# Weight sums of two Strassen projections: written to HBM ahead of time, or added in place in SBUF by accumulating transfers

## The chip, the cores and the metric

The kernel runs on one core of a Trainium2 chip. The metric is the device time of one execution in microseconds (us). The engines are named as in the profile: PE (TensorE, matmuls), DVE (VectorE), ACT (ScalarE), POOL (GpSimd) and SP (SyncE, which only issues transfers here). Each engine works through its own instructions in order and waits for others by semaphores. A transfer that POOL issues goes through the queue that the profile calls software_dynamic; one that SP issues goes through a hardware_dynamic queue.

## The reference, cut to what matters

The kernel computes one decoder block in float32, with 1024 tokens and a model width of 1024. Two mixers (an SSD branch and a gated linear attention branch, GLA) are each projected up, gated and added; the sum goes through w_o and is added to x. Then a cross attention begins with a projection through w_xq.

```python
y_ssd = ssd_mixer(z, xBC, dt_raw, ...)
y_gla = gla_mixer(q, k, v, r, a1, ...)
merged = sigmoid(g_ssd) * (y_ssd @ w_up_ssd) + sigmoid(g_gla) * (y_gla @ w_up_gla)
h = h + merged @ w_o
q = rmsnorm(h, norm_xattn) @ w_xq        # then scores against the memory, softmax, w_xo, the FFN
```

The change touches `merged @ w_o` and the product with `w_xq`, and what runs ahead of them.

## The kernel before

**Matmuls.** A float32 product is made from three matmuls of float32r parts: each operand is split into a high part (rounded by ACT) and a low part (DVE subtracts the high one), and hi x hi, hi x lo and lo x hi are added in PSUM. Arrays lie with the features on the 128 partitions and the tokens along the free side, in two token halves of 512.

**The order of the work.** A tile scheduler sets each engine's order from the program, by its own estimate of times and by priorities; code under `ahead()` is pulled forward, transfers wrapped in `pinned` keep the program's order. Stages here: the w_in projections beside the GLA chunks (`run(singles(...), (gla, ...))`, to about 803 us), dense(0) (y_ssd through w_up_ssd), dense(1) (y_gla through w_up_gla, to 986.8), the w_o product (`wo.steps()`), and the w_xq product (`xq.steps()`). `run` takes a step of each side generator per main step at a given rate.

**GLA.** There are 8 chunks. The last step of each, `norm`, transposes the chunk on PE (`bank<-ident,o`), copies it by ACT into `qk` and stores it by SP to HBM (`yg_d<-qk`). dense(0) first reads `hl<-ys_d` and its weights `raw<-in_w_up_ssd`, which ACT and DVE split into `wd`; the second `wd` buffer lies in memory that GLA's last `qk` held, so its split waits for that store. ACT also evaluates gates (`whi`, `wlo` loaded from `gs_d`).

**Wide.** The class `Wide` does a 1024 x 1024 x 1024 product by seven products of quarters (Strassen-Winograd). Each product is 48 matmuls of 128x512, in two halves of 24 that have an operand pair each (`ws`: a weight part and an activation part, both split into hi and lo). The left operand of B11, B21 and T4 is a quarter of W; those of T1, B22, T2 and T3 are sums of quarters, which the kernel has made ahead of time in HBM: `weight_sums` issues 12 transfers on POOL (copies first, then `accum_op=ALU.add` in halves of 512 KB), for w_o into `wos_d` during the GLA stage and for w_xq into `xqs_d` during dense(1). `Wide.load` then reads all seven left operands by SP as blocks of 1 MB (`wr`), three from W and four from the sums. `prep` forms the activation sums on DVE (`rq`) and splits both operands; `steps` runs three operand pairs ahead of PE; `evac` adds each product into `wk` on DVE, and for finished rows calls `post`: `post_wo` stores the row, scales it for w_xq (`put_xq`, ACT) and sums its square (`Stats.take`: ACT squares, POOL or DVE adds into `ssum`). `post_yg`, called for each of the 16 row blocks of dense(1), gates the row and adds the SSD part on POOL (`rq<-..,ga`), which yields w_o's activations.

Of the kernel before, what the change touches and what calls it, by code (L numbers as in the profile page):

```python
# [78 lines left out]
def block_kernel(ctx: ExitStack, tc: tile.TileContext, t: dict, out: bass.AP):  # L79
# [38 lines left out]
    wos_d = dram("wos_d", 2 * D, HALF)  # L118
    xqs_d = dram("xqs_d", 2 * D, HALF)
# [1101 lines left out]
    class Wide:  # L1221
# [4 lines left out]
        SEQ = ("B11", "T1", "B22", "T2", "B21", "T3", "T4")  # L1226
        LEFT = {"B11": (0, 0), "B21": (0, 1), "T1": 0, "B22": 3, "T2": 1, "T3": 2, "T4": (1, 1)}
# [5 lines left out]
        def __init__(s, W, sums_d, post, keys, side, base=None, scale=1.0, two=None):  # L1233
            s.W, s.sums_d, s.post, s.keys, s.side, s.base, s.scale = W, sums_d, post, keys, side, base, scale
            s.two = two or (lambda ap: DVE)
            s.q, s.raw, s.ops, s.keep, s.chain = {}, [], [], {}, None
# [18 lines left out]
        def home(s, i, j):  # L1255
            if (i, j) not in s.keep:
                k = s.keep[i, j] = slot(s.side[len(s.keep)], (P, 4, HALF), name="wk")
                if s.base is not None:
                    pinned(SP.dma_start(k, s.base[half(i), half(j)].rearrange("(u p) c -> p u c", p=P)))
            return s.keep[i, j]  # L1260

        def prep(s, n, pin=None):
            pin = pin or (lambda x: x)
            while len(s.ops) < min(n, 14):
                m, kp = divmod(len(s.ops), 2)
                s.load(m + 1)
                name, c = s.SEQ[m], slice(2 * kp, 2 * kp + 2)
                x = [slot("op", (P, 2, 2, HALF), F32R, name="ws") for _ in range(2)]
                with ahead():
                    if name in s.COMB:  # L1270
                        f, *q = s.COMB[name]
                        o, a, b = (s.quad(*ij)[:, c] for ij in q)
# [634 lines left out]
```

## Time and profile before

| What | us |
| --- | --- |
| Median of 3 runs | 1937.14 |
| Lowest and highest of them | 1934.5, 1938.31 |
| The profiled execution, its own time | 1939.03 |
| Its span in the trace | 1937.3 |
| PE busy in it | 1898.9 (98%) |
| DVE, ACT, POOL busy | 1359.5, 882.1, 533.6 |

All durations below are from that one profiled execution, whose own time is 1.9 us above the median of the runs. A row of a timeline gives when an operation started, how long it took, and in brackets how long its engine had stood before it and what ended that. Windows give the busy time of each engine in a stretch, the share of full speed that PE's clock was granted, and how busy the DMA engines were (1.0 is all 16; a row can come out a little above it).

### The profile page before, as it was taken

What the parts mean: (1) busy time and instruction counts of PE and PEld (TensorE: products, weight loads), DVE (VectorE), ACT (ScalarE), POOL (GpSimd) and SP (SyncE); (2) the same over time, 40 slices, a digit from 0 to 9 for tenths busy, and PEclk for the clock granted to TensorE, in tenths of its full rate; (3) what the DMA queues carried; (4) which work ended last, traced back from release to release, by engine and by line L of the source; (5) the groups of instructions that cost most, each with busy time, mean ns of one, the idle gap of its engine ahead of it and who ended that gap; (6) DMA issues with size and microseconds to landing.
All of it is one profiled execution on the core that took longest, in us unless ns stands there. A gap on an engine that the chain in (4) does not pass through costs nothing.

```text
span 1937.3 us, 26098 instructions
## 1 busy us (share of the span) xinstructions
PE 1898.9 (98%) x9680; PEld 1600.8 (83%) x9680; DVE 1359.5 (70%) x1935; ACT 882.1 (46%) x1521; POOL 533.6 (28%) x426
## 2 busy tenths in 40 slices
PE   7999999999999999899999999999999999999998
PEld 7998787888888888788888888888888888888888
DVE  7765879877776665552288685687878877866566
ACT  7534564555553444652236564553333333345243
POOL 0012324345443322001322100016544534330002
PEclk9999999999999999899999999999999999999999
DMA  9433383456653966984874420424675557397463
GB/s 343 145 94 102 126 303 117 146 164 183 185 163 121 271 193 182 338 288 161 227 202 159 170 85 12 156 94 130 181 194 147 147 166 182 101 298 264 159 222 121
DMA packets 242915, 341.04 MB, mean 176 GB/s; under 512 B 16458, under 2 KB 147764, under 8 KB 242788
## 3 DMA queue, kind: packets, MB, share of 16 engines
q1 hardware_dynamic: 225572, 293.23, 45.0%
q0 software_dynamic: 15488, 39.85, 9.8%
q10 hardware_dynamic: 1728, 6.29, 0.8%
q8 instruction: 76, 1.25, 0.3%
q14 instruction: 51, 0.42, 0.1%
HBM read 249.87 MB, written 129.30 MB: 196 GB/s over the span
## 4 chain that ended last, share of the span: by engine, by line
PE 85%; DVE 7%; DMA 3%; issue 2%; ACT 1%; POOL 1%; SPq 0%; POOLq 0%; DVEq 0%; ACTq 0%
PE acc L51 69%; PE bank L51 14%; DVE cv L73 2%; PE bank L55 2%; DVE wlo L73 2%; DVE o L73 1%; DVE hs L73 1%; DMA yg_d<-qk 1%; DMA hl<-ys_d 0%; DMA qk<-q_d 0%; DMA raw<-in_w_ffn_in_dram 0%; DMA down_d<-in_w_ffn_out_dram 0%; POOL ssum L73 0%; ACT cv L778 0%; DVE gy L73 0%
## 5 line engine op out<-in xcount | busy, mean ns | idle before, releaser
L73 DVE TENSOR_TENSOR wlo<-raw,whi 128x512 fp32r<-128x512 f32 x272 | 243.6, 903 | 97.3 <-ACT whi L233 97.3
L233 ACT ACTIVATE whi<-raw 128x512 fp32r<-128x512 f32 x272 | 169.7, 630 | 253.1 <-PE acc L51 208.8
L51 PE MATMUL acc<-hl,wd 128*128 128x512 f32 x1152 | 266.9, 393 | 6.5 <-ACT wd L233 6.5
L51 PEld LDWEIGHTS acc<-hl,wd 128*128 128x128 f32 x1152 | 217.7, 190 | 54.0 <-ACT wd L233 8.3
L73 DVE TENSOR_TENSOR o<-acc,o 128x512 f32<-128x512 f32 x244 | 166.9, 684 | 82.2 <-PE acc L51 80.5
L51 PE MATMUL acc<-fs 128*128 128x512 f32 (+1 forms) x792 | 155.7, 355 | 0.1
L51 PEld LDWEIGHTS acc<-fs 128*128 128x128 f32 x792 | 130.7, 189 | 20.8 <-issue 0.5
L73 DVE TENSOR_TENSOR fs<-fr,fs 128x1024 fp32r<-128x1024 f32 (+1 forms) x78 | 93.0, 1225 | 36.2 <-ACT fs L233 36.1
L233 ACT ACTIVATE fs<-fr 128x1024 fp32r<-128x1024 f32 (+1 forms) x78 | 74.1, 983 | 94.4 <-PE acc L51 29.2
L73 POOL TENSOR_TENSOR sa<-raw 128x512 f32<-128x512 f32 x42 | 68.3, 1625 | 149.2 <-DMA raw<-in_w_in_dram 80.3
L233 ACT ACTIVATE whi<-sa 128x512 fp32r<-128x512 f32 x96 | 59.7, 626 | 96.1 <-PE acc L51 90.5
L51 PE MATMUL acc<-ws 128*128 128x512 f32 x384 | 88.8, 390 | 0.0
L73 POOL TENSOR_TENSOR raw<-raw,sa 128x512 f32<-128x512 f32 x33 | 44.8, 1357 | 155.7 <-DVE wlo L73 155.7
L51 PEld LDWEIGHTS acc<-ws 128*128 128x128 f32 x384 | 71.9, 188 | 15.2 <-DVE ws L73 0.3
L73 DVE TENSOR_TENSOR wlo<-sa,whi 128x512 fp32r<-128x512 f32 x96 | 72.7, 757 | 8.4 <-ACT whi L233 7.5
L51 PE MATMUL acc<-T4h,whi 128*128 128x512 f32 x192 | 75.9, 395 | 2.6 <-DVE o L73 2.6
L51 PE MATMUL acc<-T3h,whi 128*128 128x512 f32 x192 | 75.7, 394 | 2.0 <-DVE o L73 2.0
L51 PE MATMUL acc<-B22h,wlo 128*128 128x512 f32 x192 | 75.8, 395 | 1.6 <-DVE wlo L73 1.6
L73 POOL TENSOR_TENSOR rstd<-rstd,mhalf 128x4 f32<-128x4 f32 (+1 forms) x7 | 8.7, 1250 | 247.8 <-DVE rstd L73 247.8
L51 PE MATMUL acc<-T1h,whi 128*128 128x512 f32 x192 | 76.3, 397 | 0.0
L51 PE MATMUL acc<-T2h,whi 128*128 128x512 f32 x192 | 75.8, 395 | 0.0
L51 PE MATMUL acc<-B22h,whi 128*128 128x512 f32 x192 | 75.7, 394 | 0.0
(420 smaller groups left out, 5039.2 us busy)
## 6 DMA issues: line engine op xcount, KB each, us to landing
raw<-in_w_in_dram SPq DMA_DIRECT2D x26, 1024.0 KB, 7.8
raw<-in_w_ffn_in_dram SPq DMA_DIRECT2D x22, 1024.0 KB, 6.7
act_d<-o SPq DMA_DIRECT2D x77, 256.0 KB, 3.3
fr<-act_d SPq DMA_DIRECT2D x35, 512.0 KB, 5.6
down_d<-in_w_ffn_out_dram POOLq DMA_DIRECT2D x18, 768.0 KB, 7.3
fr<-down_d SPq DMA_DIRECT2D x20, 512.0 KB, 4.1
ga<-h_d SPq DMA_DIRECT2D x32, 256.0 KB, 6.8
csb<-cs_d SPq DMA_DIRECT2D x15, 512.0 KB, 4.2
```

The costliest lines, as they stand in the source:

```text
L51: return s.e.matmul(o, x, y, **kw)
L55: return s.e.transpose(o, x, i)
L73: return f(*a, **kw)
L233: pin(ACT.activation(hi, src, AF.Copy))
```

## The change

The HBM buffers `wos_d` and `xqs_d` and the 24 transfers that filled them are gone from the GLA stage and from dense(1). Each `Wide` now loads five blocks by SP: B11's, B21's, T1's, T3's and T4's. Where a left operand is a sum, POOL adds another quarter of W onto a loaded block in SBUF by accumulating transfers, each in two halves of 512 KB (`plus`). T1's block A10 gets A11 at once. T2's sum is made in T1's buffer, each half after T1's split of that half has read it; B22's in the same buffer after T2's split; T3's block A00 gets A10 in a buffer of its own. The products run in a new order, B11, B21, T1, T2, B22, T3, T4; for w_o the two token halves change roles (`flip=1`); buffers have other homes. The 16 additions of `post_yg` move from POOL to DVE. The side generator of cross attention (`xq_side`) waits three steps instead of two.

```diff
-    wos_d = dram("wos_d", 2 * D, HALF)
-    xqs_d = dram("xqs_d", 2 * D, HALF)
...
-    def dense_sums(w, d):
-        return weight_sums([(t[w].rearrange("(j k p) c -> j p k c", j=2, p=P), d, 4, 0)])
-
     gla = gla_steps()
-    wsums = dense_sums("w_o", wos_d)
-    run(singles(gs[2:] + gg[:3], B, gg[3:]), (gla, 8 * 5 / 30), (wsums, 0.37), prio=PRIO)
+    run(singles(gs[2:] + gg[:3], B, gg[3:]), (gla, 8 * 5 / 30), prio=PRIO)
     drain(gla)
-    drain(wsums)
...
-        SEQ = ("B11", "T1", "B22", "T2", "B21", "T3", "T4")
-        LEFT = {"B11": (0, 0), "B21": (0, 1), "T1": 0, "B22": 3, "T2": 1, "T3": 2, "T4": (1, 1)}
+        SEQ = ("B11", "B21", "T1", "T2", "B22", "T3", "T4")
+        LEFT = {"B11": (0, 0), "B21": (0, 1), "T1": (1, 0), "T3": (0, 0), "T4": (1, 1)}
+        PLUS = {"T1": (1, 1), "T2": (0, 0), "B22": (0, 1), "T3": (1, 0)}
...
-        def load(s, n):
-            while len(s.raw) < min(n, 7):
-                src = s.LEFT[s.SEQ[len(s.raw)]]
-                if isinstance(src, tuple):
-                    i, j = src
-                    w = s.W[half(j), half(i)]
-                else:
-                    w = s.sums_d[half(src), :]
-                r = slot(s.keys[len(s.raw)], (P, 4, HALF), name="wr")
-                pinned(SP.dma_start(r, w.rearrange("(k p) c -> p k c", p=P)))
-                s.raw.append(r)
...
+        def block(s, i, j):
+            return s.W[half(j), half(i)].rearrange("(k p) c -> p k c", p=P)
+
+        def plus(s, name, k):
+            r = s.raw[name][:, k:k + 2]
+            pinned(POOL.dma_start(r, s.block(*s.PLUS[name])[:, k:k + 2], accum_op=ALU.add))
+
+        def load(s, *names):
+            for name in names:
+                if name in s.raw:
+                    continue
+                r = s.raw[name] = slot(s.keys.get(name, s.keys["*"]), (P, 4, HALF), name="wr")
+                pinned(SP.dma_start(r, s.block(*s.LEFT[name])))
+                if name in s.PLUS:
+                    for k in (0, 2):
+                        s.plus(name, k)
...
         def prep(s, n, pin=None):
...
                 m, kp = divmod(len(s.ops), 2)
-                s.load(m + 1)
                 name, c = s.SEQ[m], slice(2 * kp, 2 * kp + 2)
+                if name in s.LEFT:
+                    s.load(name)
...
+                if name in ("T1", "T2"):
+                    s.raw[s.SEQ[m + 1]] = s.raw[name]
+                    s.plus(s.SEQ[m + 1], 2 * kp)
                 s.ops.append(x)
...
-            first = name in ("B11", "T1", "B22")
+            first = name in ("B11", "T1", "T2")
...
                 for kp in range(2):
-                    s.load(m + 3)
+                    if 2 * m + kp in (0, 7):
+                        s.load("T4" if m else "T3")
                     s.prep(x + 3)
...
         gated(g, p)
-        q = wo.quad(o // 4, j)[:, o % 4]
-        add(POOL, q, g, y)
+        add(DVE, wo.rows(o, j), g, y)
...
-    wo = Wide(t["w_o"], wos_d, post_wo, ("aux",) * 7, ("m", "m", "m", "aux"), xT_d, 0.5)
+    wo = Wide(t["w_o"], post_wo, {"B21": "m", "*": "aux"}, {(0, 0): "m", (0, 1): "m", (1, 1): "m", (1, 0): "aux"}, xT_d, 0.5, flip=1)
...
-    wsums = dense_sums("w_xq", xqs_d)
-    run(dense(1, i_yg, post_yg, lambda o, j: (gate(gg_d, o, j), quad(ysg_d, o * P, 0, j))), (wide_side(wo, 8, 4, pinned), 1.0), (wsums, 0.8))
-    drain(wsums)
-    run(wo.steps(), (wide_side(xq, 7, 2), 1.0))
+    run(dense(1, i_yg, post_yg, lambda o, j: (gate(gg_d, o, j), quad(ysg_d, o * P, 0, j))),
+        (wide_side(wo, (("T1", 8), ("B11", 10), ("B21", 12)), (13, 14), pinned), 1.0))
+    run(wo.steps(), (wide_side(xq, (("T1", 6), ("B11", 7), ("B21", 8)), (11, 12)), 1.0))
```

The scheduler moves work at places far from the edit, too. On SP's queue at the end of GLA and the start of dense(0) these rows stand, first before, then in the changed kernel (L numbers are lines of each file; `hl`, `raw`, `whi`, `wlo` are loads for dense(0), `yg_d<-qk` is GLA's last store):

```order
L1396 DMA hl<-ys_d 128x1024
L1334 DMA raw<-in_w_up_ssd_dram 128x8x256 x2
L1396 DMA hl<-ys_d 128x1024 x6
L478 DMA gg_d<-o 128x512
L1450 DMA whi<-gs_d 128x512
L1450 DMA wlo<-gs_d 128x512
L1334 DMA raw<-in_w_up_ssd_dram 128x8x256
L1153 DMA yg_d<-qk 128x8x128
L478 DMA gg_d<-o 128x512
L1450 DMA whi<-gs_d 128x512
```

```order
L1413 DMA hl<-ys_d 128x1024
L1351 DMA raw<-in_w_up_ssd_dram 128x8x256
L1413 DMA hl<-ys_d 128x1024
L1351 DMA raw<-in_w_up_ssd_dram 128x8x256
L1413 DMA hl<-ys_d 128x1024 x4
L1157 DMA yg_d<-qk 128x8x128
L1413 DMA hl<-ys_d 128x1024 x2
L482 DMA gg_d<-o 128x512
L1351 DMA raw<-in_w_up_ssd_dram 128x8x256
L1467 DMA whi<-gs_d 128x512
L1467 DMA wlo<-gs_d 128x512
```

The last `yg_d<-qk` has moved ahead of the last two `hl` loads, a `gg_d` store, the third `raw` and the first two gate loads.

ACT at the same place, before and after (`qk<-bank` are the copies that feed that store, `wd<-raw` dense(0)'s first weight splits, `whi<-whi` and `wlo<-wlo` the gates):

```order
L1398 ACTIVATE hl<-hl,cols 128x1024
L1151 ACTIVATE qk<-bank 128x4x128 x2
L1398 ACTIVATE hl<-hl,cols 128x1024 x3
L1454 ACTIVATE whi<-whi 128x512
L1454 ACTIVATE wlo<-wlo 128x512
L233 ACTIVATE wd<-raw 128x1024 x2
L1454 ACTIVATE whi<-whi 128x512
```

```order
L1155 ACTIVATE qk<-bank 128x4x128 x2
L1415 ACTIVATE hl<-hl,cols 128x1024
L231 ACTIVATE whi<-raw 128x512
L362 ACTIVATE o<-acc 128x512
L1415 ACTIVATE hl<-hl,cols 128x1024 x4
L231 ACTIVATE wd<-raw 128x1024 x2
L1415 ACTIVATE hl<-hl,cols 128x1024 x2
L1471 ACTIVATE whi<-whi 128x512
L1471 ACTIVATE wlo<-wlo 128x512
```

The first two `wd` splits stood behind all `hl` and the first two gates; they now stand ahead of the last two `hl` and of every gate. On PE, 28 matmuls of 128x512 stood between the last chunk's transposes and dense(0); now 49 do.

POOL from the end of dense(1) into the w_o stage, before and after, with buffer numbers (`wr_8543` is the buffer of T1, T2 and B22, `wr_8782` that of T3, `wr_9045` belongs to w_xq; `ssum` is the sum of squares):

```order
L73 TENSOR_TENSOR rq_8561<-whi_8463,ga_8600 128x512
L73 DMA xqs_d_83<-in_w_xq_dram 128x2x512
L73 TENSOR_TENSOR rq_8595<-wlo_8464,ga_8630 128x512
L73 DMA xqs_d_83<-xqs_d_83 128x2x512
L73 TENSOR_TENSOR rq_8595<-gates_7635,ga_8663 128x512
L73 DMA xqs_d_83<-xqs_d_83 128x2x512
L73 TENSOR_TENSOR rq_8561<-gates_7635,ga_8696 128x512
L73 TENSOR_TENSOR ssum_7633<-ssum_7633,sq_9082 128x512
L73 TENSOR_TENSOR ssum_7633<-ssum_7633,sq_9094 128x512
```

```order
L73 DMA wr_8543<-in_w_o_dram 128x2x512 x2
L73 DMA wr_8782<-in_w_o_dram 128x2x512 x2
L73 DMA wr_8543<-in_w_o_dram 128x2x512 x2
L73 TENSOR_TENSOR ssum_7619<-ssum_7619,sq_8927 128x512
L73 TENSOR_TENSOR ssum_7619<-ssum_7619,sq_8939 128x512
L73 DMA wr_8543<-in_w_o_dram 128x2x512 x2
L73 DMA wr_9045<-in_w_xq_dram 128x2x512 x2
L73 TENSOR_TENSOR ssum_7619<-ssum_7619,sq_9159 128x512
L73 TENSOR_TENSOR ssum_7619<-ssum_7619,sq_9171 128x512
```

Before, transfers for w_xq and dense(1)'s additions alternate, and only `ssum` additions stand in the w_o stage. Now the transfers of T1, T3, T2 and B22 stand there in this order, two each, and two `ssum` additions between T2's and B22's. T2's wait for T1's splits on DVE, and the second `ssum` addition waits for a DVE `ssum` row that stands behind T2's two splits, T1's first evacuation and one activation split.

## Rows read from the trace of the kernel before

**Rows 1.** The page, busy time of PE: us, share of the span, instructions

```profile
PE 1898.9 (98%) x9680; PEld 1600.8 (83%) x9680; DVE 1359.5 (70%) x1935; ACT 882.1 (46%) x1521; POOL 533.6 (28%) x426
```

**Rows 2.** Windows: PE, PEld, DVE, ACT, POOL busy; granted clock, DMA share, GB/s

```profile
755.00:765.00 10.00, 8.02 (x39) 6.77 (x38) 7.42 (x19) 5.22 (x11) 2.89 (x3) 0.83 0.54 142
755.90:761.50 5.60, 3.62 (x17) 3.33 (x16) 5.56 (x14) 3.28 (x8) 0.83 (x2) 0.70 0.68 234
800.00:810.00 10.00, 5.13 (x17) 3.33 (x16) 6.25 (x6) 4.51 (x5) 0.00 (x0) 0.79 1.04 350
810.00:820.00 10.00, 8.84 (x29) 7.09 (x30) 1.47 (x2) 6.38 (x10) 0.00 (x0) 0.70 1.03 399
900.00:985.00 85.00, 85.00 (x377) 70.38 (x376) 29.40 (x29) 18.51 (x22) 28.27 (x24) 1.00 0.76 216
985.00:1000.00 15.00, 15.00 (x68) 12.43 (x67) 15.00 (x11) 5.82 (x7) 4.99 (x4) 1.00 0.98 307
1010.00:1020.00 10.00, 10.00 (x45) 8.25 (x44) 9.03 (x12) 2.61 (x3) 0.00 (x0) 1.00 0.01 2
```

**Rows 3.** PE's timeline: start, us, operation, idle ahead of it and what ended it

```profile
757.89 0.61 PE L51 MATMUL acc<-T3h,whi 128*128 128x512 f32 x1 [1.98 <-DVE o L73]
...
806.74 2.07 PE L51 MATMUL acc<-hl,wd 128*128 128x512 f32 x4 [3.68 <-ACT wd L233]
811.16 175.77 PE L51 MATMUL acc<-hl,wd 128*128 128x512 f32 x764 [2.35 <-ACT wd L233]
...
986.77 11.04 PE L51 MATMUL acc<-ws 128*128 128x512 f32 x48
997.65 11.04 PE L51 MATMUL bank<-ws 128*128 128x512 f32 x48
```

**Rows 4.** ACT's timeline at the seam between GLA and dense(0)

```profile
805.11 0.63 ACT L1454 ACTIVATE wlo<-wlo 128x512 f32<-128x512 f32 x1 [0.18 <-DMA wlo<-gs_d]
805.65 1.04 ACT L233 ACTIVATE wd<-raw 128x1024 fp32r<-128x1024 f32 x1
810.05 1.06 ACT L233 ACTIVATE wd<-raw 128x1024 fp32r<-128x1024 f32 x1 [3.36 <-DMA yg_d<-qk]
```

**Rows 5.** The chain of waits at the seam: start, us, what

```profile
798.99 10.98 DMA yg_d<-qk
```

**Rows 6.** DMA issues: operation, count, size, median us to landing; all to `xqs_d`

```profile
wr<-wos_d SPq DMA_DIRECT2D x4, 1024.0 KB, 5.4
DMA to landing us min/median/max: 5.6/6.9/9.2
```

**Rows 7.** DVE's and POOL's timelines, four operations

```profile
750.70 1.23 DVE L73 SCALAR_TENSOR_TENSOR qk<-qk,e 128x512 f32<-128x512 f32 x1 [6.28 <-DMA qk<-q_d]
...
991.27 1.21 DVE L73 TENSOR_TENSOR ws<-wr,ws 128x1024 fp32r<-128x1024 f32 x1
992.41 0.68 DVE L73 SCALAR_TENSOR_TENSOR gates<-gates,acc 128x512 f32<-128x512 f32 x1
...
1033.57 1.30 POOL L73 TENSOR_TENSOR ssum<-ssum,sq 128x512 f32<-128x512 f32 x1 [34.93 <-ACT sq L519]
```

**Rows 8.** POOL's timeline, transfers that follow one another

```profile
755.89 0.84 POOL L73 DMA_DIRECT2D wos_d<-in_w_o_dram  x1
761.54 1.16 POOL L73 DMA_DIRECT2D wos_d<-in_w_o_dram  x1 [4.81 <-issue]
...
936.37 1.18 POOL L73 DMA_DIRECT2D xqs_d<-in_w_xq_dram  x1 [6.88 <-issue]
...
942.79 1.15 POOL L73 DMA_DIRECT2D xqs_d<-in_w_xq_dram  x1 [2.69 <-issue]
...
979.49 1.19 POOL L73 DMA_DIRECT2D xqs_d<-in_w_xq_dram  x1 [3.95 <-issue]
...
986.63 1.16 POOL L73 DMA_DIRECT2D xqs_d<-xqs_d  x1 [4.62 <-issue]
...
996.14 1.17 POOL L73 DMA_DIRECT2D xqs_d<-xqs_d  x1 [7.02 <-issue]
```

More of the change, by code (lines that the diff above doesn't have):

```diff
@@ L457, in run, with waiting @@
                         next(g, None)
+    def waiting(g, n):
+        for _ in range(n):
+            yield
+        for _ in g:
+            yield
     def chain(gs):
@@ L1231, in block_kernel, with __init__ @@
         OUT = {"B11": (0, 0), "T1": (1, 1), "B22": (0, 1), "T2": (0, 1), "B21": (0, 0), "T3": (1, 1), "T4": (1, 0)}
[L1233 to L1236, printed above, removed]
+        def __init__(s, W, post, keys, side, base=None, scale=1.0, flip=0):
+            s.W, s.post, s.keys, s.side, s.base, s.scale = W, post, keys, side, base, scale
+            s.q, s.raw, s.ops, s.keep, s.full, s.chain, s.flip = {}, {}, [], {}, set(), None, flip
         def quad(s, i, j):
@@ L1241, in quad, with rows, home @@
             return s.q[i, j]
-        def load(s, n):
-            while len(s.raw) < min(n, 7):
-                src = s.LEFT[s.SEQ[len(s.raw)]]
-                if isinstance(src, tuple):
-                    i, j = src
-                    w = s.W[half(j), half(i)]
-                else:
-                    w = s.sums_d[half(src), :]
-                r = slot(s.keys[len(s.raw)], (P, 4, HALF), name="wr")
-                pinned(SP.dma_start(r, w.rearrange("(k p) c -> p k c", p=P)))
-                s.raw.append(r)
[L1255 to L1260, printed above, removed]
+        def rows(s, o, h):
+            return s.quad(o // 4, h ^ s.flip)[:, o % 4]
+        def block(s, i, j):
[12 more added lines that the diff above has]
+                        s.plus(name, k)
+        def home(s, *ij, fill=True):
+            if ij not in s.keep:
+                s.keep[ij] = slot(s.side[ij], (P, 4, HALF), name="wk")
+            if fill and s.base is not None and ij not in s.full:
+                s.full.add(ij)
+                i, j = ij
+                pinned(SP.dma_start(s.keep[ij], s.base[half(i), half(j ^ s.flip)].rearrange("(u p) c -> p u c", p=P)))
+            return s.keep[ij]
         def prep(s, n, pin=None):
@@ L1297, in steps @@
                 if name in ("B11", "T1", "B21"):
-                    banks = [(acc if name == "B11" else bank)() for _ in range(4)]
+                    other = [(acc if name == "B11" else bank)() for _ in range(4)]
                     if name == "B11":
-                        s.chain = banks
-                elif name in ("T2", "T3", "T4"):
-                    banks = s.chain
+                        s.chain = other
+                banks = s.chain if name in ("T2", "T3", "T4") else other
                 fresh = name in ("B11", "T1", "B21")
-                if s.base is not None:
-                    for z in s.SEQ[m:m + 2]:
+                if m == 0:
+                    for ij in s.side:
+                        if ij != (1, 0):
+                            s.home(*ij, fill=False)
+                for z in s.SEQ[m:m + 2]:
+                    if z != "T4" or s.base is not None:
                         s.home(*s.OUT[z])
                 for kp in range(2):
-                    s.load(m + 3)
+                    if 2 * m + kp in (0, 7):
+                        s.load("T4" if m else "T3")
                     s.prep(x + 3)
@@ L1463, in post_yg, with post_wo, wide_side @@
         gated(g, p)
[L1464 to L1486 removed]
+        add(DVE, wo.rows(o, j), g, y)
+    def post_wo(o, h, q, last):
+        SP.dma_start(h1_d[o * P:(o + 1) * P, half(h)], q)
+        put_xq(o, h, q, col("norm_xattn", o))
+        s1.take(h, q)
+    wo = Wide(t["w_o"], post_wo, {"B21": "m", "*": "aux"}, {(0, 0): "m", (0, 1): "m", (1, 1): "m", (1, 0): "aux"}, xT_d, 0.5, flip=1)
+    def wide_side(x, plan, ops, pin=None):
+        for n in range(16):
+            x.load(*(name for name, at in plan if at == n))
+            if n in ops:
+                x.prep(ops.index(n) + 1, pin)
+            yield
     def residual(store, stats, gain, put, scale=1.0):
@@ L1534, in xq_side @@
     def xq_side():
-        for _ in range(2):
+        for _ in range(3):
             yield
```

32 lines of the change are left out of this document (6 added, 26 removed).

## The prediction

> **What bounds the kernel now.** I read the page first: TensorE (PE) is busy for 98% of the span [rows 1]. So an edit is worth only what it takes from PE's few losses, or adds to them. I read the windows second, for those losses [rows 2]; PE's own rows third, for what ends them [rows 3]. Two places lie near the change.
>
> At the seam between the GLA stage and dense(0), 800 to 820, PE does 17 and 29 matmuls in two windows of 10 us [rows 2]. One product of 48 matmuls takes 997.65 - 986.77 = 10.88 us at full clock [rows 3], 0.227 us each, so 20 us hold 88. 46 were done: 42 x 0.227 = **9.5 us** are lost. The gaps, 3.68 and 2.35 us, both end on the split of `wd` in ACT [rows 3]. The rest is the clock: the granted clock is 0.79 and 0.70 in these windows, so that PE ran a part of them at the lower level, 1.2 GHz; it fell after PE had stood for 3.68 us [rows 2, 3]. Why the splits are late: the first (805.65) stands in ACT behind the two gate activations, which wait for their loads (805.11 is the second) [rows 4]; the second waited until 809.97 for the last store `yg_d<-qk`, since `wd` lies where `qk` was. That store was issued at 798.99 and took 10.98 us [rows 5], with the DMA engines at 1.04 and 1.03 [rows 2].
>
> At 755.9 PE stands for 1.98 us for a DVE sum [rows 3]; DVE itself had waited 6.28 us for a load `qk<-q_d` [rows 7]. The clock is 0.83 over the window of 10 us: 10 x 0.17 = 1.7 us [rows 2]. Together **3.7 us**.
>
> In the two Wide stages themselves PE has nothing to give back: it runs product after product, 10.88 us each, and its windows are full [rows 2, 3]. There a new wait is a pure loss.
>
> **The change part by part.** *(1) The sums of w_o leave the GLA stage.* 12 POOL transfers between 630.4 and 790.8 go, and with them 8 MB of copies and accumulations. Where they go the scheduler packs GLA's last chunk otherwise: in SP's order the last `yg_d<-qk` stands ahead of two `hl` loads, a weight block and the gate loads, instead of behind them. That is two loads of 512 KB, one block of 1 MB, two gates and a `gg_d` store of 256 KB each, 2.75 MB. At the 350 GB/s of this stretch [rows 2] 2.75 MB are 7.9 us of queue. In ACT the two `wd` splits stand ahead of the last two `hl` and of all gate activations. On PE 49 instead of 28 large matmuls (that is by counting the rows of the order) follow the last chunk's transposes: 21 x 0.227 = 4.8 us of cover. So the store may be issued about 4.8 us earlier (794.2) and, with up to 7.9 us less ahead of it, take some 6 to 10 us: it lands at 800 to 804, where PE comes to need the second split at about 804. After it one split in ACT (1.04, [rows 4]) and one in DVE remain, so I leave a gap of 1.2 us and no drop of the clock: gain 9.5 - 1.2 = **8.3 us**. Bounds: 9.5, if nothing remains; 3, if the DMA engines, full at 1.03 in any order, keep a gap of 3 us and its slow clock.
>
> *(2) The 3.7 us at 755.9.* DMA engines carry less there without the sums, but the loads of w_in stay. The row shows only that DVE waited for a load, not that POOL's transfers delayed it. Bounds 0 and 3.7; I take half, **1.8 us**.
>
> *(3) The sums of w_xq leave dense(1), and 16 adds `rq<-` go from POOL to DVE.* PE loses nothing in 900 to 985 now, so nothing is gained. The adds cost DVE 16 x 0.68 us (a 128x512 DVE row [rows 7]) = 10.9 us; DVE is busy 29.40 of 85 us there [rows 2], which hides them. At 985 to 1000 DVE is full (15.00); three adds may fall there, 2 us, beside PE's first product of 10.88 us whose operands are then ready. I set 0; without this cover, up to 10.9 us lost.
>
> *(4) Stores and reloads of sums in HBM go, five blocks are loaded and four added in place.* On SP's queue two 1 MB loads per Wide fewer. Beside PE that is not a gain.
>
> *(5) The sums now form inside the Wide stage, on POOL's queue.* This is the cost. POOL's rows show that one of its transfers starts only when the one before is done: ahead of the later one of a pair POOL stands 4.81, 2.69, 4.62 and 7.02 us on "issue", which the page calls a wait for nothing that it shows [rows 8]; the beats that follow are a little above these transfers' times to landing, 5.6 to 9.2 us [rows 6]. I call the time from one start to the next the beat, c. Rows: 5.65 for a plain copy of 1 MB (755.89 to 761.54); for accumulations of 512 KB 6.42 (936.37 to 942.79), 7.14 (979.49 to 986.63) and 9.51 (986.63 to 996.14) [rows 8]. In POOL's order T1's halves come first, then **both halves of T3**, then T2's two, then two `ssum` adds, then B22's two. T3 is needed after B22, yet stands ahead.
>
> With PE's start at 986.8 and 5.44 us per half product, T2's halves are needed at 986.8 + 6 x 5.44 = 1019.4 and 1024.9, B22's at 1030.3 and 1035.7. T3's block is issued at about 987 and in at 994 (5.4 us is the median for such a load [rows 6]; I add some, since the engines are at 0.98 [rows 2]). Behind that the chain runs: T2's halves are in at 994 + 3c and 994 + 4c; a split takes 1.04 in ACT and 1.21 in DVE, 2.3 us [rows 4, 7]. The second `ssum` add waits for a DVE row that stands behind T2's second split, T1's first evacuation and one more split: about 2.2 us, and 1.30 us for the add itself [rows 7], 3.5 in all. B22's halves follow at c each.
> At c = 6.2: T2 at 1014.9 and 1021.1, in time; `ssum` over at 1024.6; B22 at 1033.1 (2.8 late) and 1039.3 (0.8 more): 3.6 us.
> At c = 7.14: T2 at 1017.7 and 1024.9, in time; `ssum` 1028.4; B22 at 1037.8 (7.5 late) and 1045.0 (1.8 more): 9.3 us.
> At c = 9.51: T2 5.4 and 4.1 late, B22 about 10 and 4: 23 us.
> For w_xq the same chain without the `ssum` adds ahead of B22 starts 76 us later: 0 us at 6.2, about 5.6 at 7.14, 20 at 9.51.
> DRAM to SBUF accumulation stands in no row. Its nearest rows are the DRAM to DRAM ones above, of the same size and run length. From 1010 to 1020 the DMA engines are at 0.01 [rows 2], so I take a beat between the two shortest rows, nearer to the accumulation's, c = 6.2, and price one drop of the clock behind the stall at 1.7 us as at 755.9: 3.6 + 1.7, **5.3 us** lost. Bounds: 0 (c = 5.65, where by the same sum B22 would be some 0.5 late) and 43 (c = 9.51 in both).
>
> *Sum:* -8.3 - 1.8 + 5.3 = **-4.8 us**: the profiled execution's 1939.03 us (1937.3 of them its span) become 1934.2. That execution is 1.9 above the median of the runs, 1937.14; there I predict **1932.3**.
>
> **The rivals.**
> *A: the chain of transfers stalls PE (slower).* It decides at the beat: with c = 6.5 the loss (5.4 us in w_o, 1.7 in w_xq, one or two drops of the clock) eats the 10.1 us of gain. At c = 7.14 the loss is 9.3 + 5.6 + two drops of 1.7 = 18.3: +8, 1945; at 9.51 it is 43 and two drops, about +36, 1973. For it: 9.51 was measured in 985 to 1000, the start of this very stage, with DVE busy 15.00 of 15.00 us [rows 2, 8]. Against it: the DMA share was 0.98 there, too. The 5.65 was measured with DVE just as full, 5.56 of 5.60 us, at a share of 0.68 [rows 2, 8]. So the beat goes with the load of the DMA engines, and from 1010 they are empty.
> The Trainium skill, "SBUF — State Buffer", section "SBUF: two separate sides", says the opposite for some DVE operations: a POOL transfer's descriptors are written by GpSimd, which a DVE operation that holds the shared port keeps from it. Were that so for the two-input operations that fill DVE here, every transfer beside them would have the beat of 9.51, and the time would be A's 1973; the window of 5.56 of 5.60 speaks against it, and A keeps its chance from the full engines at the stage's start.
> *B: no stall and the full gain.* If beats stay at 5.65 and both losses vanish, 9.5 + 3.7 = 13.2: 1924. For it: the empty DMA engines; against: PE's first `wd` at the seam still needs a store to land.
> The Trainium skill, "DMA: Bandwidth & Descriptors", section "Anatomy of one DMA — SWDGE (gpsimd) path", gives about 2.0 us plus the bytes at 436 GB/s for a POOL transfer, an estimate of 3.2 us for 512 KB. By it no half would be late and B would hold; no accumulation's beat here comes near it, the shortest shown being 6.42.
> *C: the seam only moves (no change).* The engines are full at 800 to 820 in either order, the gap stays at 3 us with its slow clock (gain 3), and the halves cost 5.3: 1937.14 + 2.3, 1939.
>
> **How the numbers follow.** Forecast (gain 8 to 11, loss 2 to 7; 1928 to 1936): 0.45. A: 0.23. B: 0.12. C: 0.20. What a measurement can tell from no change is 0.2%, 3.9 us: faster is below 1933.3, slower above 1941.0. Faster: B and most of the forecast, 0.12 + 0.40 = 0.52. Slower: most of A and a little of C, 0.23. Same: 0.25. The range runs from B's 1924 to A at c of about 7.5, 1950; A beyond that (0.1) and what lies below B (0.04) are left out.
>
> **What the profile would show.** (1): PE's gaps at the start of `acc<-hl,wd` under 1.5 us in sum, the clock at 1.00 there, and `yg_d<-qk` landing before the end of GLA's matmuls. (2): no PE gap on a DVE `o` some 45 us before that. (5): POOL transfers `wr<-in_w_o` about 6 us apart, and PE's stall in the w_o stage at B22's first half, ended by a split that waited for such a transfer; none in w_xq. Wrong would be the forecast if the beat is over 6.5, if PE's loss at the seam stays over 6 us, or if DVE's 16 adds delay an evacuation in dense(1).

## The result and the profile after

The changed kernel takes 1946.0 us (median of 7 runs, 1944.16 to 1947.04); the kernel before, on the same chip, 1938.01 (7 runs). The ratio is 1.004, 95% interval 1.0028 to 1.0051: **8 us slower**. The forecast was 4.8 us faster, 1932.3. The time lies in the range, 1924 to 1950, and next to rival A, 1945.

PE is busy for as great a share as before [rows 1]. It is busy 3.8 us longer, and it also stands 4.2 us longer (1945.3 us of span less 1902.7 busy, against 1937.3 less 1898.9). The page of the changed kernel, busy us of each engine:

```profile
PE 1902.7 (98%) x9680; PEld 1601.1 (82%) x9680; DVE 1354.4 (70%) x1946; ACT 880.2 (45%) x1521; POOL 518.3 (27%) x407
```

The windows that answer to [rows 2] (same columns) show that the gain came. The clock is 1.00 at 755, and 800 to 820 hold 36 + 46 = 82 matmuls instead of 46:

```profile
755.00:765.00 10.00, 10.00 (x46) 8.50 (x45) 3.32 (x8) 3.85 (x13) 3.26 (x3) 1.00 0.24 79
800.00:810.00 10.00, 8.46 (x36) 6.48 (x36) 7.26 (x7) 6.13 (x8) 0.00 (x0) 1.00 1.06 394
810.00:820.00 10.00, 10.00 (x46) 8.29 (x45) 3.25 (x5) 7.47 (x11) 0.00 (x0) 1.00 1.04 401
```

PE's timeline of the changed kernel shows where it went again (start, us, operation, idle ahead of it and what ended it):

```profile
801.26 2.13 PE L51 MATMUL acc<-hl,wd 128*128 128x512 f32 x8 [1.15 <-ACT wd L231]
...
976.23 4.92 PE L51 MATMUL acc<-ws 128*128 128x512 f32 x21
...
1026.79 8.93 PE L51 MATMUL bank<-ws 128*128 128x512 f32 x28 [6.87 <-ACT ws L231]
...
1085.69 3.04 PE L51 MATMUL bank<-ones,ssum 128*128 128x1 f32 x16 [1.90 <-DVE wk L73]
...
1149.47 7.23 PE L51 MATMUL acc<-kvhl,hl 128*128 128x256 f32 x58
```

The w_o stage starts at 976.23 instead of 986.77 [rows 3]: **10.5 us gained**. The first matmul of the scores, behind both Wide stages, starts at 1149.47. Before it started at 1141.12:

```profile
1141.12 7.12 PE L51 MATMUL acc<-kvhl,hl 128*128 128x256 f32 x58
```

So the two Wide stages take 1149.47 - 976.23 = 173.2 us instead of 154.4: **18.9 us lost** there. 10.5 - 18.9 = -8.4 is the whole result. The gaps of this stretch are 6.87 us ahead of B22's first half, 1.90 at the matmuls for the statistics, and five small ones of 0.20 to 0.75 from 1107 to 1138 in the w_xq stage, 2.5 in sum. That is 11.3. About 5.9 more is the clock. It is 0.50, the lower level, in 1025 to 1031.7, where PE had stood for 6.87 us, and again in 1086.31 to 1093.13, after PE had stood for 1.90 us and had begun matmuls with only one column. The 28 matmuls behind the first gap take 8.93 us, 2.4 more than at the full clock; the 16 single-column ones take 3.04, 1.2 more than the 1.84 before; the 48 behind them take 13.29, 2.25 more than a product's 11.04 [rows 3]. The last 1.7 us of the 18.9 are not traced to a place.

```profile
988.00:994.70 6.70, 6.70 (x31) 5.56 (x30) 6.67 (x7) 1.41 (x2) 1.23 (x2) 1.00 0.50 79
1014.70:1025.00 10.30, 5.22 (x24) 3.98 (x22) 3.16 (x5) 0.27 (x1) 1.30 (x3) 0.99 0.96 291
1025.00:1031.70 6.70, 4.91 (x12) 3.86 (x13) 2.36 (x2) 2.00 (x3) 1.21 (x2) 0.50 0.48 79
1067.91:1074.84 6.93, 6.93 (x33) 5.72 (x32) 6.93 (x7) 6.93 (x11) 6.93 (x1) 1.00 0.87 276
1086.31:1093.13 6.82, 6.82 (x23) 5.85 (x24) 3.93 (x8) 1.85 (x3) 1.21 (x1) 0.50 0.48 77
1091.30:1098.00 6.70, 6.70 (x27) 5.46 (x26) 0.00 (x0) 0.21 (x1) 1.21 (x1) 0.86 0.53 78
```

What PE waited for at 1026.79 is followed through three engines. ACT's split there waited 11.28 us for a POOL transfer:

```profile
1024.73 1.06 ACT L231 ACTIVATE ws<-wr 128x1024 fp32r<-128x1024 f32 x1 [11.28 <-DMA wr<-in_w_o_dram]
```

POOL's timeline shows the chain that [rows 8] only let one guess at:

```profile
981.48 1.21 POOL L73 DMA_DIRECT2D wr<-in_w_o_dram  x1 [31.17 <-DMA wr<-in_w_o_dram]
987.96 1.22 POOL L73 DMA_DIRECT2D wr<-in_w_o_dram  x1 [5.27 <-issue]
994.65 1.21 POOL L73 DMA_DIRECT2D wr<-in_w_o_dram  x1 [5.47 <-DVE rq L73]
1001.69 1.21 POOL L73 DMA_DIRECT2D wr<-in_w_o_dram  x1 [5.83 <-issue]
...
1014.75 1.22 POOL L73 DMA_DIRECT2D wr<-in_w_o_dram  x1
1024.97 1.21 POOL L73 DMA_DIRECT2D wr<-in_w_o_dram  x1 [9.00 <-issue]
...
1067.91 8.09 POOL L73 TENSOR_TENSOR ssum<-ssum,sq 128x512 f32<-128x512 f32 x1 [7.97 <-ACT sq L523]
1076.08 1.29 POOL L73 TENSOR_TENSOR ssum<-ssum,sq 128x512 f32<-128x512 f32 x1
1077.31 1.19 POOL L73 DMA_DIRECT2D wr<-in_w_xq_dram  x1
...
1091.30 1.21 POOL L73 DMA_DIRECT2D wr<-in_w_xq_dram  x1 [5.38 <-issue]
1098.01 1.22 POOL L73 DMA_DIRECT2D wr<-in_w_xq_dram  x1 [5.49 <-issue]
```

T3's two transfers (981.48, 987.96) stand ahead of T2's (994.65, 1001.69), then come two `ssum` additions (1010.33 and 1013.53, each waiting for a square from ACT), then B22's halves (1014.75, 1024.97). The beats are 6.48, 6.69, 7.04 and then, for B22's first half, **10.22 us**. SP's timeline shows what ran beside that one: five loads of 1 MB issued from 1004.81 to 1014.4, for w_o's residual and last product and w_xq's first three (the first and the last two are shown):

```profile
1004.81 0.46 SPq L1268 DMA_DIRECT2D wk<-xT_d  x1
...
1013.48 0.92 SPq L1257 DMA_DIRECT2D wr<-in_w_xq_dram  x2
```

The DMA share is 0.96 in 1014.7 to 1025. The row of 0.01 that I had gone by, 1010 to 1020 in the kernel before [rows 2], is not the same stretch of the stage: it lies 23 to 33 us behind the stage's first matmul, and B22's first half ran 39 to 49 us behind it. In the w_xq stage T3's pair starts at 1077.31, behind two `ssum` additions. The first took 8.09 us, where one takes 1.30 [rows 7]; DVE worked without a break for its first 6.93 us (the window of 1067.91). The second took 1.29, with DVE standing.

### The profile page after: what moved, and what is told of

It is laid out like the page before. It is cut to its first block, busy times and chain, and to the rows that moved or that the text cites. A ratio compares the mean times of both kernels' runs of the same rounds, so it can differ in the third digit from the quotient of the medians.

```text
span 1945.3 us, 26091 instructions
## 1 busy us (share of the span) xinstructions
PE 1902.7 (98%) x9680; PEld 1601.1 (82%) x9680; DVE 1354.4 (70%) x1946; ACT 880.2 (45%) x1521; POOL 518.3 (27%) x407
## 5 line engine op out<-in xcount | busy, mean ns | idle before, releaser
L51 PE MATMUL bank<-ws 128*128 128x512 f32 x288 | 72.0, 409 | 8.3 <-ACT ws L231 7.1
```

Source lines behind the costliest of these rows:

```text
L51: return s.e.matmul(o, x, y, **kw)
```

## The experiments

My theory after this look (**Q**): the loss is the order on POOL's queue, which does one transfer at a time. Rivals: **S**, that the `ssum` additions on POOL are what delays B22; **L**, that SP's loads beside a transfer are; and for the gain, that it has another cause than the transfers taken out of the GLA stage. Each kernel ran beside the kernel before on the same chip; the ratios are against that. "Start" is the first w_o matmul, "Wide" the time from there to the first matmul of the scores, both from the profile.

| Kernel | Ratio, 95% interval | Start | Wide |
| --- | --- | --- | --- |
| before | 1 | 986.8 | 154.4 |
| the changed kernel | 1.0040 (1.0028 to 1.0051) | 976.2 | 173.2 |
| T3 last (e1) | 1.0006 (0.9996 to 1.0016) | 974.3 | 168.9 |
| ssum on DVE (e2) | 1.0013 (1.0004 to 1.0021) | 976.4 | 170.2 |
| both (e3) | 0.9982 (0.9972 to 0.9992) | 974.2 | 163.9 |
| before, w_o's sums in dense(0) (e4) | 0.9958 (0.9944 to 0.9973) | 981.3 | 154.2 |
| changed, sums put back into GLA (e5) | 1.0087 (1.0070 to 1.0104) | 986.1 | 173.5 |
| e4, sums held until 818 (e6) | 1.0028 (1.0019 to 1.0038) | 983.3 | 161.6 |
| e3, SP's loads later (e7) | 0.9993 (0.9984 to 1.0003) | 975.4 | 167.4 |
| changed, SP's loads later (e8) | 1.0065 (1.0051 to 1.0080) | 975.3 | 182.3 |
| e3, some loads later (e9) | 0.9996 (0.9986 to 1.0006) | 974.6 | 166.5 |
| e1, some loads later (e9b) | 1.0019 (1.0010 to 1.0028) | 976.3 | 170.8 |
| before, sums at 0.7 per step (e10) | 1.0040 (1.0025 to 1.0054) | 997.6 | 154.2 |
| before, sums at 1.0 per step (e11) | 1.0039 (1.0023 to 1.0054) | 993.0 | 154.9 |

### The order on POOL and the additions (e1, e2, e3)

T3 last, and the additions of the first statistics on DVE:

```diff
-                if name in s.PLUS:
+                if name == "T1":
                     for k in (0, 2):
                         s.plus(name, k)
...
                     s.plus(s.SEQ[m + 1], 2 * kp)
+                    if name == "T2" and kp:
+                        for k in (0, 2):
+                            s.plus("T3", k)
```

```diff
-    s1 = Stats(rp, "ga", 6)
+    s1 = Stats(rp, "ga", 6, DVE)          # Stats.take then adds on DVE, not on either(q)
```

> The changed kernel with one edit: T3's two accumulating transfers are issued after B22's instead of ahead of T2's, in both Wide stages. In the changed kernel the stretch from the first w_o matmul to the first matmul of the scores takes 173.2 us against 154.4 before, so 18.9 us are lost there, while its start came 10.5 us earlier. Theory Q (the order on POOL's one-at-a-time queue makes the stall): T2's and B22's halves start up to two beats (13 us) earlier, PE's 6.9 us stall at B22 and the small stalls of the w_xq stage go, 3 to 5 us of the 18.9 remain (a 1.9 us gap at the statistics matmuls and its slow clock); time 1930 to 1933. Rival L (the loads that SP issues at 1004 to 1014 hold B22's first half, whose beat was 10.2 us): the stall only moves, over 4 us of it stay, 1939 or more. Rival S (the two ssum additions ahead of B22 on POOL are what delays it): nearly unchanged, 1942 to 1946.

> The changed kernel with one edit: the additions of the squares for the first statistics (ssum) all run on DVE, none on POOL, so that B22's halves follow T2's directly; T3's halves still stand ahead. Theory Q: B22's first half starts at about 1008 instead of 1014.75, and is in 0 to 1 us late; the stall of 6.9 us and its slow clock go, the small stalls of the w_xq stage stay; 1935 to 1938. Rival S: all of the stall and the gap of 1.9 us at the statistics go, 1929 to 1932. Rival L: the first half meets the loads of 1004 to 1014 all the same and takes 10 us, 1938 to 1942.

> The changed kernel with both edits: T3's transfers after B22's, and the ssum additions on DVE. Theory Q and rival S alike: no stall in either Wide stage, the 10.5 us gained ahead of it remain, 1926 to 1930, faster than the kernel before. Rival L: 1934 or more, with a stall behind whatever transfer meets the loads.

Each edit alone brought back a part: 4.3 and 3.0 us of the 18.9 in the Wide stages (173.2 to 168.9 and 170.2); both together 9.3, to 163.9, and a kernel 0.18% faster than before. So Q and S are both part of the cause and neither is all of it: the three times missed the numbers of Q and of S on the slow side. L's numbers hold in e1 (1942.39 us) and e3 (1936.44), e2 (1944.0) lies above all that were written for it, and in all three kernels B22's first half takes a long beat (10.54, 10.72 and 10.76 us), as L said. POOL and PE of the kernel with T3 last:

```profile
1004.42 1.21 POOL L73 DMA_DIRECT2D wr<-in_w_o_dram  x1
1014.96 1.21 POOL L73 DMA_DIRECT2D wr<-in_w_o_dram  x1 [9.33 <-issue]
...
1021.05 5.76 PE L51 MATMUL bank<-ws 128*128 128x512 f32 x24 [2.14 <-DVE ws L73]
...
1029.89 2.07 PE L51 MATMUL acc<-ws 128*128 128x512 f32 x4 [3.08 <-ACT ws L231]
```

T2's halves start at once (980.45 and 989.72), but B22's first half meets the same loads and takes a beat of 10.54 us (1004.42 to 1014.96). T3's first half, behind that beat, is 3.08 us late: the stall has moved and shrunk, as L said. The gap of 2.14 us is another matter. It is in B22's first half, whose transfer had landed by 1014.7 and which ACT had split by 1016.7; DVE's split of it stands behind four evacuations of T2's product, which wait for PE, and ends at 1020.99. With the additions on DVE as well it is again DVE that is late. POOL, then DVE and PE of that kernel:

```profile
997.01 1.21 POOL L73 DMA_DIRECT2D wr<-in_w_o_dram  x1 [6.22 <-DVE ws L73]
1007.77 1.21 POOL L73 DMA_DIRECT2D wr<-in_w_o_dram  x1 [9.55 <-PE bank L51]
1017.24 1.21 POOL L73 DMA_DIRECT2D wr<-in_w_o_dram  x1 [8.26 <-issue]
1023.89 1.21 POOL L73 DMA_DIRECT2D wr<-in_w_o_dram  x1 [5.45 <-issue]
```

```profile
1041.19 2.30 DVE L73 TENSOR_TENSOR ssum<-ssum,sq 128x512 f32<-128x512 f32 x3
1043.41 1.28 DVE L73 SCALAR_TENSOR_TENSOR wk<-acc,wk 128x512 f32<-128x512 f32 x2
...
1044.24 6.19 PE L51 MATMUL acc<-ws 128*128 128x512 f32 x14 [4.63 <-DVE wk L73]
```

Both of B22's beats are long (10.76 and 9.47), T3's second half starts at 1023.89, and DVE, which splits it and then has T4's splits and three `ssum` additions in its queue, comes to T3's evacuation at 1043.41 only. T4 adds onto the same PSUM banks, so PE stands 4.63 us. Of the 9.5 us that are still lost in e3, this gap is 4.63, one of 1.53 ahead of w_xq's T4 (1126.82) comes on top, and 2.9 are the clock behind the first: 96 matmuls take 24.80 us there, 21.9 at full clock.

### The loads beside the transfers (e7, e8, e9, e9b)

```diff
-                    if 2 * m + kp in (0, 7):
+                    if 2 * m + kp in (0, 9):
...
-    run(wo.steps(), (wide_side(xq, (("T1", 6), ("B11", 7), ("B21", 8)), (11, 12)), 1.0))
+    run(wo.steps(), (wide_side(xq, (("T1", 9), ("B11", 10), ("B21", 10)), (11, 12)), 1.0))
```

(e7 and e8, of which e7 ran first; in e9 and e9b T1 stays at 6, with B11 at 9 and B21 at 10. L2 is the theory that a beat is 6.6 us by itself and grows only beside SP's loads; D, that evacuations come late behind the additions on DVE.)

> The changed kernel with only SP's loads later, as in the run before this one; T3's halves still ahead, ssum additions on POOL. Theory L2 and Q together: B22's first half still starts at about 1014, but is in after 6.6 instead of 10.2 us, so PE's stall shrinks from 6.9 to about 3.5 us and the clock drop stays: 1942 to 1944. If the loads are all of the stall: 1936 to 1939.

> The changed kernel with T3's transfers last and the ssum additions on DVE, as in the run with both, and SP's loads for T4 and for w_xq's first three products asked for later (T4 at the tenth half product instead of the eighth, w_xq's T1 three steps later, B11 three, B21 two). In the run with both, B22's halves took beats of 10.8 and 9.5 us beside 5 MB of these loads, T3's halves came late and PE stood 4.6 us ahead of T4. Theory L2 (the beat is 6.6 us by itself and grows only beside SP's loads): B22's beats fall to 6.5 to 8, the gap ahead of T4 goes, and the time is 5 to 7 us below that run: 1929 to 1932 beside 1938 for the kernel before. Rival D (DVE as the longer chain: with the ssum additions on it, evacuations come late whatever the loads do): the gap stays, 1934 to 1937.

> The changed kernel with T3's transfers last and the ssum additions on DVE, and only those loads later that are not needed soon: T4 at the tenth half product instead of the eighth, w_xq's B11 and B21 at the tenth and eleventh; w_xq's T1 stays where it is, so that its sum is made in time. Theory L2: B22's halves meet 2 to 3 MB of loads instead of 5, T3's halves come some 5 us sooner, the 4.6 us gap ahead of T4 goes, and no new wait arises behind w_xq's T1 as in the runs with T1 later; 6 us below the run with both edits: 0.994 to 0.996 of the kernel before. Rival D (ssum additions on DVE hold the evacuations whatever the loads do): the gap of 3 to 5 us stays, 0.997 to 0.999.

> As the run before it, with the ssum additions left where the scheduler put them (most on POOL). Theory: the run with T3 last alone lost 2.1 and 3.1 us at B22 and T3, behind one beat of 10.5 us beside the loads; with the loads spread that beat is 7 to 8 and both stalls nearly go; the gap of 1.9 us at the statistics, behind two POOL additions that took 9.5 us, stays: 0.997 to 0.999 of the kernel before. If the ssum additions on POOL are what holds the halves, it stays at 1.000 to 1.001.

For the stall that it aimed at, e8 came out as theory L2 said; its time, 1953.48 us against 1942 to 1944, did not. POOL, DVE and PE of e8:

```profile
1013.76 1.20 POOL L73 DMA_DIRECT2D wr<-in_w_o_dram  x1
1020.37 1.21 POOL L73 DMA_DIRECT2D wr<-in_w_o_dram  x1 [5.42 <-issue]
...
1060.46 1.22 POOL L73 DMA_DIRECT2D wr<-in_w_xq_dram  x1 [9.33 <-issue]
...
1064.35 0.69 DVE L73 TENSOR_TENSOR ssum<-ssum,sq 128x512 f32<-128x512 f32 x1 [13.51 <-POOL ssum L73]
...
1022.20 0.79 PE L51 MATMUL bank<-ws 128*128 128x512 f32 x1 [3.20 <-ACT ws L231]
...
1071.47 13.39 PE L51 MATMUL acc<-ws 128*128 128x512 f32 x48 [12.61 <-DVE wk L73]
```

B22's first half takes 6.61 us (1013.76 to 1020.37), and PE's stall ahead of it falls from 6.87 to 3.20 us, with one of 0.66 behind it that ends on DVE's split. That is the price of the loads: 3.0 to 3.6 us of stall, and 3.6 us of the beat of 10.2. But the kernel as a whole became slower still, by a stall that I had not expected: w_xq's T1 now comes late, its two transfers (1049.92, 1060.46) stand in POOL's queue ahead of an `ssum` addition, DVE waits 13.51 us for that addition, and PE 12.61 us for an evacuation behind it. In e7, and in e9, where T1 kept its place, the gap ahead of T4 stayed (3.25 and 3.98 us), as rival D said. But e9b, with the additions back on POOL, has a gap of 5.03 us there, so that additions on DVE are not what makes it; that DVE's queue has T4's splits ahead of the evacuation of T3 remains, and is not shown. Nor did e7 and e9 free B22's first half: its beat is 10.59 beside 2 MB of loads and four stores in e7, and 10.72 beside 3 MB of loads in e9. e9b's is 8.16. All four kernels were slower than the numbers written for them, e7 1939.47 us against 1929 to 1937 and e9 and e9b just above their ranges. So moving loads takes back in one place what it gives in another; no version with in-place sums that I tried comes below 0.9982.

### Where the gain came from (e4, e5, e6, e10, e11)

e5 puts the 12 transfers back into the changed kernel, and e4 takes them out of the GLA stage of the kernel before, into dense(0), where POOL does nothing:

```diff
-    wsums = dense_sums("w_o", wos_d)
-    run(singles(gs[2:] + gg[:3], B, gg[3:]), (gla, 8 * 5 / 30), (wsums, 0.37), prio=PRIO)
+    run(singles(gs[2:] + gg[:3], B, gg[3:]), (gla, 8 * 5 / 30), prio=PRIO)
     drain(gla)
-    drain(wsums)
...
+    wsums = dense_sums("w_o", wos_d)
-    run(dense(0, ...), (fetch_gated(yg_d, sr_d, i_yg), 1.0))
+    run(dense(0, ...), (fetch_gated(yg_d, sr_d, i_yg), 1.0), (waiting(wsums, 4), 1.0))
+    drain(wsums)
```

> The changed kernel with the 12 transfers of w_o's sums put back into the GLA stage (they fill a buffer in HBM that nothing reads any more); the Wide stages are the changed kernel's. With them the scheduler sets the seam as before: the last yg_d store behind the last hl loads and the gate loads. If taking these transfers out of the GLA stage gave the 10.5 us, they are lost again: w_o starts at 985 to 988 in the profile instead of 976, time 1954 to 1957. If the gain came from elsewhere (additions on DVE, less traffic in dense(0) and dense(1)), it stays at 1945 to 1947.

> The kernel before with one edit: w_o's 12 transfers for the sums run during dense(0), where POOL has nothing to do, instead of during the GLA stage; the Wide stages are as before. If the 10.5 us that the changed kernel gained ahead of the w_o stage come from taking these transfers out of the GLA stage (with the order at the seam that follows), this kernel gains them too and loses nothing: 1927 to 1930. If they come from anything else in the change (additions moved to DVE, less traffic in dense(0) and dense(1)), it stays at 1936 to 1938. If the transfers in dense(0) hold its own loads up, some of it is lost again: 1930 to 1936.

e5 lost 9.9 of the 10.5 us: start at 986.1, Wide as in the changed kernel. PE and windows of e5 show both places again, the gap behind DVE at 758 and 16 + 32 = 48 matmuls in 800 to 820:

```profile
758.53 0.47 PE L51 MATMUL acc<-T3h,whi 128*128 128x512 f32 x1 [2.16 <-DVE o L73]
...
800.00:810.00 10.00, 4.18 (x16) 2.85 (x16) 6.10 (x6) 5.49 (x7) 0.00 (x0) 0.91 1.03 340
810.00:820.00 10.00, 9.16 (x32) 7.44 (x33) 1.91 (x2) 6.51 (x10) 0.00 (x0) 0.75 1.00 375
```

So the gain is the transfers' absence from the GLA stage, with the order that the scheduler makes without them; that is shown. e4 gained it without touching the Wide stages, but in the trace only 5.4 us of it: start 981.3, Wide 154.2. POOL, the chain of waits and PE of e4:

```profile
785.28 0.98 POOL L73 DMA_DIRECT2D wos_d<-in_w_o_dram  x1
...
789.40 13.48 DMA hl<-ys_d
...
805.05 17.33 PE L51 MATMUL acc<-hl,wd 128*128 128x512 f32 x66 [5.05 <-ACT wd L233]
```

Nothing holds POOL's transfers back on the chip, so they start at 785.28 and not when dense(0) does, and an `hl` load takes 13.48 us beside them; the seam's gap of 5.05 us is behind that load. e4 is the **fastest kernel of this study**: 0.9958 of before, 1932.36 us where before has 1940.39 in the same runs. That is the third case written for it, a gain of which the transfers beside dense(0)'s loads take a part back. Those medians lie 8.0 us apart and the two traces 5.4; the interval holds both.

> The kernel before with w_o's sums in dense(0) as in the run that put them there, and one 128x4 addition on POOL ahead of them that waits for a row of dense(0), so that POOL cannot start them at 785 beside the hl loads (there they stretched a load to 13.5 us and left a PE gap of 5 us at the seam). If that collision is what kept the gain at 5 us instead of 10, w_o starts at 976 to 978 and the time is 1926 to 1929. If the sums in dense(0) now hold up its own loads or dense(1)'s additions behind them on POOL, part of it is lost again: 1930 to 1936.

Its added line, in `post_ys`: `if (o, j) == (1, 0): pinned(POOL.tensor_tensor(hold, g[:, :4], g[:, :4], ALU.add))`. It missed. The seam was nearly free of loss, but the 12 transfers, from 818.17 on and up to 10.8 us each beside dense(0)'s loads, then reached into dense(1) (POOL and PE of e6):

```profile
913.51 1.15 POOL L73 DMA_DIRECT2D wos_d<-wos_d  x1 [4.58 <-issue]
914.23 1.74 POOL L73 TENSOR_TENSOR rq<-whi,ga 128x512 f32<-128x512 f32 x1
...
924.31 26.13 PE L51 MATMUL acc<-hl,wd 128*128 128x512 f32 x98 [4.68 <-ACT wd L233]
```

POOL's additions `rq<-`, which stood behind them, came at 914.23; the gate buffers that they free were late, and PE stood 4.68 us. The Wide stages lost 7.4 us too (161.6 against 154.2 in e4), with a gap of 4.22 us at 1009.86 that ends on a split in DVE and a slow clock behind it; why that split is late I did not follow.

> The kernel before with one number changed: w_o's transfers for the sums run at 0.7 per step of the GLA stage instead of 0.37, so that they are done well ahead of the seam at 800. The scheduler then sets the seam much as in the changed kernel: the last yg_d store ahead of four hl loads, 54 large matmuls instead of 28 behind the last transposes. If the 10.5 us come from what stands at the seam, not from having the transfers at all, w_o starts at 976 to 979 and nothing is lost in the Wide stages: 0.994 to 0.996 of the kernel before. If the denser transfers hold up w_in's loads in the GLA stage instead, new gaps at 650 to 750 take 3 to 10 us back: 0.997 to 1.001.

> The same with 1.0 per step, the transfers as early as the queue lets them. If only the seam matters, like the run before it, 0.994 to 0.996; if w_in's loads are held up, worse than it.

Both missed. The seam is without loss in them (PE 20.00 of 20 us busy in 800 to 820), but the denser transfers hold up GLA's loads. DVE and PE of e10:

```profile
744.89 4.06 DVE L73 SCALAR_TENSOR_TENSOR qk<-qk,e 128x512 f32<-128x512 f32 x1 [13.50 <-DMA qk<-q_d]
...
754.28 0.77 PE L51 MATMUL acc<-B22h,whi 128*128 128x512 f32 x1 [10.89 <-DVE o L73]
```

DVE waited 13.50 us for `qk<-q_d`, PE 10.89 us for DVE. The loss went from the seam into the GLA stage, and grew.

## Why the prediction failed, by its own steps

**(1) The seam: right.** 8.3 us were forecast. 82 instead of 46 matmuls in 20 us are 36 x 0.227 = 8.2; the gaps that remain are 1.15 us and a smaller one, against 1.2 forecast, and the clock stays at 1.00. That the gap has the forecast's size is luck: the split that ends it (800.17) stood in ACT behind four `hl` activations, and not behind the store, which was issued at 789.94 instead of 794.2.

**(2) The gap at 755.9: right in sign, half in size.** 1.8 taken, the full 3.7 gained; e5 shows the gap of 2.16 us return with the transfers. With the 8.2 of (1) that makes 11.9, and 10.5 were measured at the start of w_o: 1.4 us are lost again in small amounts, which no run explains.

**(3) Additions on DVE: right.** PE is full in 900 to 985, with DVE at 42.31 of 85.

**(5) The chain on POOL: the step that failed.** 5.3 us were forecast, 18.9 measured: 11.3 of gaps, 5.9 of clock and 1.7 that are not traced. The chain itself was the right one, and its times up to T2 were nearly the forecast's, counted from PE's start: T3's first half starts 5.3 us after it (7.2 forecast), T2's first 18.4 (19.6 forecast). Three terms of the sum were mis-sized:
- *The beat of B22's first half.* I took 6.2 for the whole chain, because the DMA engines stood at 0.01 in 1010 to 1020 [rows 2]; 10.22 was measured. That row was the wrong stretch already in the kernel before. By my own sum at 6.2 B22's halves run from 1024.6 to 1037.0, and there the engines stand at 0.22 and 0.83:

```profile
1024.60:1030.80 6.20, 6.20 (x29) 5.15 (x28) 3.15 (x5) 3.48 (x5) 0.00 (x0) 1.00 0.22 85
1030.80:1037.00 6.20, 6.20 (x29) 5.15 (x28) 5.76 (x6) 4.97 (x8) 1.59 (x2) 1.00 0.83 278
```

The change then moved SP's loads as well: they come 28.6 to 38.2 us into the stage, just ahead of B22's first half and beside it, where the kernel before had its last ones 45 to 56 us in. I had worked out POOL's order for this stage, but not SP's. e8 prices the difference at 3.0 to 3.6 us of PE's stall. The other beats of both stages, 6.5 to 7.4 and 6.8 in the mean, were 0.6 above my 6.2.
- *The w_xq stage.* I gave it 0. T3's pair starts at 1077.31, about 8 us later after the stage's start than I had set, behind two POOL additions of 8.09 and 1.29 us; the statistics' gap of 1.9 us, the five small ones and a second drop of the clock follow.
- *The clock.* One drop of 1.7 us was priced; there were two, of 2.4 and about 3.5 us.

**The rivals.** A was the result, and its mechanism was the right one: at a beat of 7.14 it gave 18.3 us of loss and 1945. That its price agrees so well is partly luck: its 18.3 are 14.9 of late halves and 3.4 of clock, where 11.3 of gaps and 5.9 of clock were measured, with one beat of 10.22 among others of 6.8 in the mean. It had 0.23, against 0.45 for a forecast that lay one row away. My 6.2 lay below all three accumulations in [rows 8], and A's point of decision, 6.5, below two of them; a forecast that needs a beat under the lowest of these rows for six transfers one behind the other in w_o, and again in w_xq, was not the likelier one. B came out wrong by the loss, and C by the seam, which kept no gap of 3 us.
The rule that I had set beside A, from the Trainium skill's "SBUF — State Buffer", section "SBUF: two separate sides" (a POOL transfer's descriptors are held up while a DVE operation of certain kinds holds the shared port), does not show for the two-input operations that fill DVE here: the beat from 987.96 is 6.69 us with DVE busy 6.67 of 6.70 us, the one from 1091.30 is 6.71 with DVE at 0.00. The Trainium skill's lock between DVE and POOL instructions, in the same section, by which one that holds the shared port blocks the other fully, agrees with another row: of the two `ssum` additions the one of 8.09 us had a busy DVE beside it for 6.93, the one of 1.29 a standing DVE.
The price that I had set beside B, an estimate of 3.2 us for 512 KB from the Trainium skill's "DMA: Bandwidth & Descriptors", section "Anatomy of one DMA — SWDGE (gpsimd) path", was far off here: no accumulating transfer of this size into SBUF had a beat under 6.4.

**Still open.** How the 18.9 us divide between the causes is known only by halves, since the edits interact: T3's place 4.3, the additions 3.0, together 9.3, the loads 3.0 to 3.6 for one stall; 9.5 us remain in e3. The gap ahead of T4 in them is read from the trace as DVE's queue, but no run changed that queue's order alone. That a busy DVE is what stretched the POOL addition to 8.09 us rests on its stretch of time alone; no run took DVE's work away from beside it.

## What to carry to other kernels

Work that is taken out of one stage and put into another has to be costed against the new stage as it will be, with all the loads that the same change brings there; an empty window of the old trace says nothing of it, least of all one that lies at another time of the stage than the new work will. A queue that serves one transfer at a time is a chain like an engine: write down its order, give each entry the ordinary beat (6.8 us here) and not the best, put first what is needed first, and keep short additions that others wait for off it. Before such a change, look for the smaller edit that gets the gain alone: here moving 12 transfers to another stage gave 0.42%, and the rebuilt product, at best, 0.18%.

## What the runs showed of the hardware

An accumulating transfer of 512 KB into SBUF takes a beat of 6.5 to 7.1 us on POOL's queue when little else moves, with DVE idle or full (6.71 and 6.69 us), and 8.2 to 10.8 beside 2 to 5 MB of SP's loads issued shortly before or during it (8.16 in e9b, 10.22 in the changed kernel, 10.76 in e3). The share of busy DMA engines does not set it alone: the transfer of 942.44 in the changed kernel took 6.62 us at a share of 1.00. A POOL addition of 128x512 that takes 1.29 us with DVE standing took 8.09 us where DVE worked without a break for its first 6.93. After PE had stood for 1.90 us and begun 16 single-column matmuls, its granted clock was 0.50 for 6.82 us; the same 16 without a wait ahead of them, in e3, left it at 1.00. A wait alone does not decide it either: one of 3.25 us in e7 (1044.67) left the clock at 1.00, one of 1.90 us in e9 (1128.46), with ordinary matmuls on both sides, brought it to 0.78 in 1128.4 to 1136.
